# Two four-branch mixers: rotary key from the token product, a narrower first chunk, and y turns in other places

## Chip, cores, metric

One core of a Trainium2 chip runs the whole program in one launch. The metric is device microseconds (us) of that core. Engines: PE is TensorE, DVE is VectorE, ACT is ScalarE, POOL is GpSimd, and SP issues the DMAs.

## What is computed

Two networks run one after the other on 256 tokens of width 1024: first a block of two layers (feed-forward, mixer, feed-forward), then a block of two layers (mixer of four branches, feed-forward). The change lies in the second block's mixers alone. With `z = h @ w_in`, cut to what matters:

```
y_a = pool_mixer(pool_u)
y_b = chunk_band_attention(ca_q, ca_k, ca_v)
y_c = dsa_attention(sa_q, sa_k, sa_v, idx_q, idx_k, idx_w)   # top 64 keys of each query
y_d = mla_attention(cq, ckv, kr)                             # latents, key's rotary part from kr
k_rope = rope(kr, pos)            # 32 columns: kr * cos + swapped(kr) * sin, same for 4 heads
x = x + gt1 * (group_rmsnorm([y_a, y_b, y_c, y_d]) @ w_out)
```

`dsa_attention` scores every key with eight index heads, keeps the best 64 of them, and gives all others a large negative score. Everything is float32. Each large product is made of three matmuls on a split of both operands into a high and a low part (hi*hTh, lo*hTh, hi*hTl).

## The kernel before

Tokens stand in two tiles of 128 (t = 0 and 1; a step's last number is t). A mixer runs as a list of steps written out by hand, `ORDER2` for both four-branch mixers. PE executes its instructions in exactly that order. The order on DVE, ACT and POOL is made by a scheduler from priorities: `^60` after a step raises that of its instructions, and `@tp`, `@dn` and `@up` name the pool of PSUM banks (2 of tp, 4 of dn, 2 of up) from which the step takes its bank.

The steps that the prediction names, with their lines in the kernel before:

- `c0.t.i`, `c4.t.i` (`gemm_tok`, L477 to L480): products by tokens; c0 holds the latents cq and ckv, sa_v and idx_w, 456 columns wide. `ch.n.i` (`gemm_ch`, L491 to L493): products by channels, four tiles of 128 channels in chunk n, 24 matmuls in each quarter i.
- `lat.t` (L1265 to L1283) normalises the latents of one token tile into `cn`: DVE sums, POOL's power (L394), DVE scalings (L1278, L1279) and two small DVE copies. `lat_turn.t` (L1285) transposes `cn` on PE and ACT copies it to `cqT`. `mla_kv` makes keys and values from it.
- `dsa_in` (L1369) takes sa_k, sa_q and the index key out of chunk 1, and makes the rotary key there: chunk 1 held kr twice and its swapped form twice as one tile of 128 channels, which L1378 to L1380 turn into `mkT[64:128]`.
- `select.t`: PE makes index scores (L1420), ACT takes relu, DVE sums eight heads (L1429, L1431), and then DVE runs eight rounds of MAX8 and MATCH_REPLACE8 (L1436, L1437) and writes the penalty `pen` (L1439), which `dsa_score.t` adds to its scores (L1447).
- `name_pv.t` (`pv`, L846, then L849 on DVE) makes one branch's output y and `y_norm` normalises it: ACT squares (L865), DVE adds eps (L866), POOL's power (L394), DVE scales (L868). `name_y_turn.t` (L887) transposes y on PE; ACT (L892 or L898) and DVE (L893, or L901 and L902) split it into high and low parts.
- `w.t.k` (`down`, L501 to L504): product with row block k of `w_out` for token tile t. Blocks 6 and 7 are branch mla's, 0 and 1 pool's, 2 and 3 ca's, 4 and 5 dsa's.
- `L289` (ACT) and `L292` (DVE) split every weight tile into high and low parts.

A y of `pv` and the tiles `sc` and `pen` of `select` come from one pool of eight buffers (`s1`).

Of the kernel before, what the change touches and what calls it, by code (L numbers as in the profile page):

```python
# [10 lines left out]
ACTF = mybir.ActivationFunctionType  # L11
# [4 lines left out]
P = 128  # L16
# [8 lines left out]
def _columns(parts):  # L25
# [80 lines left out]
class Net:  # L106
# [374 lines left out]

    def gemm_ch(self, banks, unit, i):

        nc = self.nc
        hi, lo = unit
        for c in range(4):
            out = banks[c // 2][:, (c % 2) * 256:(c % 2) * 256 + 256]
            for kk in range(2):
                k = 2 * i + kk
                sl = slice(kk * 512 + c * 128, kk * 512 + (c + 1) * 128)  # L490
                nc.tensor.matmul(out, hi[:, sl], self.hTh[:, k], start=(k == 0 and c % 2 == 0), stop=False)  # L491
                nc.tensor.matmul(out, hi[:, sl], self.hTl[:, k], start=False, stop=False)  # L492
                nc.tensor.matmul(out, lo[:, sl], self.hTh[:, k], start=False, stop=(k == 7 and c % 2 == 1))  # L493

# [421 lines left out]

    def products(self, v, ks, mod, nxt, widths):
# [323 lines left out]
    def mixer2(self, l, mod, nxt):  # L1241
# [23 lines left out]
        def lat(t):  # L1265
# [224 lines left out]
        ops["c0"] = first("c0", 456, lat_out)  # L1490
        ops["c4"] = first("c4", 512, u_out)
# [24 lines left out]
    def body(self, n_sub, whole):  # L1516
# [72 lines left out]
def _constants():  # L1589
# [47 lines left out]
def layout(inp):  # L1637
# [125 lines left out]
    krs = np.concatenate([pc["kr"][..., 16:], pc["kr"][..., :16]], -1)
    out["mix2"] = mixer([pc["cq"], pc["ckv"], pc["sa_v"], pc["idx_w"]], 456,
                        [pc["pool_u"], pc["ca_v"], pc["sa_k"], pc["idx_k"], pc["kr"], pc["kr"], krs, krs,
                         pc["sa_q"], pc["idx_q"], pc["ca_q"], pc["ca_k"]], f["w_out_2"], ORDERS[2:])

# [39 lines left out]
```

## Time and profile before

| | |
|---|---|
| median of 3 runs | 1643.0 us (1641.3 to 1643.08) |
| the profiled execution's own time | 1641.78 us |
| its span in the trace | 1640.0 us |
| PE busy in it | 1601.5 us (98%) |
| PE's mean granted clock | 0.991 of full speed |

The span is what the trace covers; the execution's own time has some 1.8 us around it. In the trace PE's matmuls overlap each other, so a matmul's own duration is longer than its share of the engine's time: what one matmul costs is read from the distance between two starts. Times in the rows count from the span's start. The first four-branch mixer takes from about 1019 to 1135 us, the second from about 1328 to 1445 us.

### The profile page before, as it was taken

Reading aid. Unit: us, or ns where it says so; the run is one execution under the profiler, and the core shown is the slowest. Engines: PE = TensorE matmul, PEld = TensorE weight load, DVE = VectorE, ACT = ScalarE, POOL = GpSimd, SP = SyncE. Lnnn points to the kernel's source line nnn. Section 1 sums busy time; section 2 is a strip of 40 time slices with the busy share of each in tenths; the row PEclk is TensorE's granted clock in tenths of the full one; section 3 lists DMA queues with packets and bytes.
Section 4 is the critical chain, followed back from the end, with each engine's and each line's share of the span. In section 5 each row is a group of like instructions: output and inputs, shape, how many; then the busy total and the mean of one; then the engine's idle time right before and its main releaser. Section 6 shows DMA issues by size and latency. Waiting matters only on the chain.

```text
span 1640.0 us, 26615 instructions
## 1 busy us (share of the span) xinstructions
PE 1601.5 (98%) x10578; PEld 1446.6 (88%) x10578; DVE 1267.4 (77%) x2163; ACT 856.3 (52%) x1372; POOL 52.5 (3%) x62
## 2 busy tenths in 40 slices
PE   7999999999999999999899999999999999999998
PEld 6989988789998899989789998987899989789997
DVE  6988698688887978777688887687888776786554
ACT  5643558564445544458564445556544465474442
POOL 0000010000000000010000000001000010000000
PEclk9999999999999999999999999999999999999999
DMA  9889777369887798844369886434888854258550
GB/s 374 304 317 372 273 256 271 116 226 364 324 320 266 294 358 320 333 162 152 115 209 371 318 319 254 174 135 149 309 331 306 331 193 150 82 179 296 184 189 27
DMA packets 60623, 410.84 MB, mean 251 GB/s; under 512 B 6785, under 2 KB 7505, under 8 KB 14290
## 3 DMA queue, kind: packets, MB, share of 16 engines
q1 hardware_dynamic: 60208, 408.85, 67.6%
q8 instruction: 83, 1.36, 0.3%
q10 hardware_dynamic: 290, 0.29, 0.1%
q14 instruction: 42, 0.34, 0.1%
HBM read 408.02 MB, written 1.09 MB: 249 GB/s over the span
## 4 chain that ended last, share of the span: by engine, by line
PE 84%; DVE 9%; ACT 3%; DMA 2%; issue 1%; POOL 1%; SPq 0%; POOLq 0%; ACTq 0%; DVEq 0%
PE up L491 13%; PE up L492 13%; PE up L493 13%; PE dn L501 8%; PE dn L502 8%; PE dn L504 8%; DVE lo L292 2%; PE dn L477 2%; PE dn L480 2%; PE dn L478 2%; PE up L477 2%; PE up L480 2%; PE up L478 2%; PE dn L584 1%; DMA s<-in_w_ada 1%
## 5 line engine op out<-in xcount | busy, mean ns | idle before, releaser
L289 ACT ACTIVATE hi<-raw 128x1024 fp32r<-128x1024 f32 (+1 forms) x508 | 526.7, 1057 | 421.4 <-PE up L492 138.1
L292 DVE TENSOR_TENSOR lo<-raw,hi 128x1024 fp32r<-128x1024 f32 (+1 forms) x508 | 609.7, 1221 | 160.9 <-ACT hi L289 157.2
L491 PE MATMUL up<-hTh,hi 128*128 128x256 f32 x1920 | 540.8, 282 | 0.0
L492 PE MATMUL up<-hTl,hi 128*128 128x256 f32 x1920 | 538.0, 280 | 0.0
L493 PE MATMUL up<-hTh,lo 128*128 128x256 f32 x1920 | 537.9, 280 | 0.0
L491 PEld LDWEIGHTS up<-hTh,hi 128*128 128x128 f32 x1920 | 361.1, 188 | 3.2 <-issue 0.2
L492 PEld LDWEIGHTS up<-hTl,hi 128*128 128x128 f32 x1920 | 361.6, 188 | 2.1
L493 PEld LDWEIGHTS up<-hTh,lo 128*128 128x128 f32 x1920 | 361.5, 188 | 0.0
L345 DVE SCALAR_TENSOR_TENSOR raw<-raw,crow 128x1024 f32<-128x1024 f32 x224 | 267.5, 1221 | 2.6 <-DMA raw<-in_w_ada 2.3
L501 PE MATMUL dn<-hi,s 128*128 128x512 f32 x552 | 218.6, 396 | 0.0
L502 PE MATMUL dn<-lo,s 128*128 128x512 f32 x552 | 217.5, 394 | 0.0
L504 PE MATMUL dn<-hi,s 128*128 128x512 f32 x552 | 173.5, 394 | 0.0
L504 PEld LDWEIGHTS dn<-hi,s 128*128 128x128 f32 x552 | 103.7, 188 | 24.4
L502 PEld LDWEIGHTS dn<-lo,s 128*128 128x128 f32 x552 | 103.8, 188 | 21.4
L501 PEld LDWEIGHTS dn<-hi,s 128*128 128x128 f32 x552 | 103.7, 188 | 21.3
L676 ACT ACTIVATE s<-up 128x512 f32<-128x512 f32 (+1 forms) x59 | 32.0, 554 | 143.8 <-PE up L493 143.6
L677 DVE TENSOR_TENSOR s<-s,up 128x512 f32<-128x512 f32 (+1 forms) x59 | 36.8, 633 | 60.7 <-PE up L493 58.7
L477 PE MATMUL dn<-hi,hTh 128*128 128x512 f32 (+2 forms) x176 | 66.2, 380 | 0.3 <-DVE hTh L431 0.3
L426 ACT ACTIVATE s<-tp,shift,scale 128x128 f32<-128x128 f32 x144 | 52.0, 466 | 26.4 <-PE tp L439 26.4
L478 PE MATMUL dn<-lo,hTh 128*128 128x512 f32 (+2 forms) x176 | 65.1, 374 | 0.0
L480 PE MATMUL dn<-hi,hTl 128*128 128x512 f32 (+2 forms) x176 | 63.4, 375 | 0.0
L394 POOL TENSOR_TENSOR rs<-ms,mhalf 128x1 f32<-128x1 f32 x22 | 20.8, 948 | 1197.5 <-DVE ms L408 1197.5
(379 smaller groups left out, 2000.5 us busy)
## 6 DMA issues: line engine op xcount, KB each, us to landing
raw<-in_ffn SPq DMA_DIRECT2D x197, 1024.0 KB, 5.0
raw<-in_w_ada SPq DMA_DIRECT2D x64, 1024.0 KB, 6.3
raw<-in_mix SPq DMA_DIRECT2D x48, 1024.0 KB, 5.1
raw<-in_w_mod SPq DMA_DIRECT2D x48, 1024.0 KB, 7.0
s<-in_w_ada SPq DMA_DIRECT2D x16, 512.0 KB, 12.6
s<-gate SPq DMA_DIRECT2D x10, 512.0 KB, 9.1
raw<-in_mix SPq DMA_DIRECT2D x4, 1032.0 KB, 8.1
raw<-in_mix SPq DMA_DIRECT2D x4, 912.0 KB, 5.8
```

The costliest lines, as they stand in the source:

```text
L289: self.line("a", nc.scalar.activation(out=hi[:, :width], in_=r, func=ACTF.Copy))
L292: self.line("v", nc.vector.tensor_tensor(lo[:, :width], r, hi[:, :width].bitcast(F32), ALU.subtract))
L345: nc.vector.scalar_tensor_tensor(sl, sl, 1.0, self.crow, ALU.mult, ALU.mult, accum_out=dst[:, b:b + 1])
L477: nc.tensor.matmul(out, xh, hi[:, sl], start=(k == 0), stop=False)
L478: nc.tensor.matmul(out, xh, lo[:, sl], start=False, stop=False)
L480: nc.tensor.matmul(out, xl, hi[:, sl], start=False, stop=(k == 7))
L491: nc.tensor.matmul(out, hi[:, sl], self.hTh[:, k], start=(k == 0 and c % 2 == 0), stop=False)
L492: nc.tensor.matmul(out, hi[:, sl], self.hTl[:, k], start=False, stop=False)
L493: nc.tensor.matmul(out, lo[:, sl], self.hTh[:, k], start=False, stop=(k == 7 and c % 2 == 1))
L501: nc.tensor.matmul(banks[t, n], xh, hi[:, sl], start=first, stop=False)
L502: nc.tensor.matmul(banks[t, n], xh, lo[:, sl], start=False, stop=False)
L504: nc.tensor.matmul(banks[t, n], xl, hi[:, n * 512:n * 512 + 512], start=False, stop=last)
```

## The change

The rotary key is made by tokens now. c0 is 32 columns wider (488) and carries kr; `lat` makes kr * cos and the swapped kr * sin with three small DVE products and adds them, four times side by side, into columns 384 to 511 of `cn`; `lat_turn` transposes this fourth tile too, and DVE copies it into `mkT[64:128]`. Chunk 1 loses the tile that held kr, and has three tiles. `dsa_in` loses its three rotary instructions. The weights' layout follows.

`ORDER2` moves `mla_pv.1` and `mla_y_turn.1` to later places, `select.1` so to an earlier one, `dsa_y_turn.0` behind `ca_pv.1`, and `dsa_y_turn.1` behind `w.1.6`. Both mixers use it.

```diff
-gate_send@dn^150 gate_fetch mla_turn.1 ch.3.2 mla_pv.1@tp select.1^60 mla_y_turn.0 ch.3.3 pool_y_turn.0^-60
-mla_y_turn.1@tp^-60 ca_in w.0.6 ca_score.0@dn w.0.7 dsa_score.0 w.0.0 ca_score.1^-25 ca_turn.0@dn^25 w.0.1
-ca_pv.0@dn^150 dsa_turn.0@tp^60 dsa_score.1^-25 w.1.1 dsa_pv.0 ca_y_turn.0@tp ca_turn.1@dn^60 w.1.0 dsa_y_turn.0@tp
-ca_pv.1@dn^60 dsa_turn.1^150 w.0.2 w.0.5 w.0.4 w.0.3 ca_y_turn.1^-150 dsa_pv.1@dn^-25 w.1.7 w.1.3 dsa_y_turn.1@up
-w.1.6 resume.0 w.1.2 w.1.5 w.1.4
+gate_send@dn^150 gate_fetch mla_turn.1 ch.3.2 select.1^60 mla_y_turn.0 ch.3.3 ca_in mla_pv.1@tp pool_y_turn.0^-60
+w.0.6 ca_score.0@dn w.0.7 dsa_score.0 mla_y_turn.1@tp^-60 w.0.0 ca_score.1^-25 ca_turn.0@dn^25 w.0.1
+ca_pv.0@dn^150 dsa_turn.0@tp^60 dsa_score.1^-25 w.1.1 dsa_pv.0 ca_y_turn.0@tp ca_turn.1@dn^60 w.1.0 ca_pv.1@dn^60
+dsa_y_turn.0@tp dsa_turn.1^150 w.0.2 w.0.5 w.0.4 w.0.3 ca_y_turn.1^-150 dsa_pv.1@dn^-25 w.1.7 w.1.3 w.1.6
+dsa_y_turn.1@up resume.0 w.1.2 w.1.5 w.1.4
...
-        for c in range(4):
+        for c in range(tiles):
...
+            rope = self.con("rope_k")[:, t * 64:t * 64 + 64]
+            kr = self.sm(64, "kr", 2)
+            nc.vector.tensor_tensor(kr[:, 0:32], ps[:, 456:488], rope[:, 0:32], ALU.mult)
+            nc.vector.tensor_tensor(kr[:, 32:48], ps[:, 472:488], rope[:, 32:48], ALU.mult)
+            nc.vector.tensor_tensor(kr[:, 48:64], ps[:, 456:472], rope[:, 48:64], ALU.mult)
+            nc.vector.tensor_tensor(cn[:, 384:512].rearrange("p (o n) -> p o n", o=4),
+                                    kr[:, 0:32].rearrange("p (o n) -> p o n", o=1).to_broadcast([P, 4, 32]),
+                                    kr[:, 32:64].rearrange("p (o n) -> p o n", o=1).to_broadcast([P, 4, 32]), ALU.add)
...
-            for c in range(3):
+            for c in range(4):
                 nc.tensor.transpose(pt[:, c * 128:(c + 1) * 128], cn[:, c * 128:(c + 1) * 128], self.ident)
...
+            nc.vector.tensor_copy(mkT[64:128, :, t * 128:(t + 1) * 128],
+                                  pt[64:128, 384:512].rearrange("p (o n) -> p o n", o=1).to_broadcast([64, 4, 128]))
...
-            return b, [(b[:, 0:456], 0, 456)]
+            return b, [(b[:, 0:488], 0, 488)]
...
-            nc.vector.tensor_tensor(k1[0:64], c1[0][0:64, 256:512], self.con("rope_k")[0:64], ALU.mult)
-            nc.vector.tensor_tensor(k2[0:64], c1[0][64:128, 256:512], self.con("rope_k")[64:128], ALU.mult)
-            nc.vector.tensor_tensor(mkT[64:128],
-                                    k1[0:64].rearrange("p (o n) -> p o n", o=1).to_broadcast([64, 4, 256]),
-                                    k2[0:64].rearrange("p (o n) -> p o n", o=1).to_broadcast([64, 4, 256]), ALU.add)
...
-                    width = (1032 if i < 6 else 912) if name == "c0" else 1024
+                    width = (1032 if i < 6 else 976) if name == "c0" else 768 if i > 5 and name == "ch1" else 1024
```

How the engines' queues change is read from the built programs. The first place is PE's queue in the first mixer, from `dsa_score.0` on, first before the change. L793 with L1447 is `dsa_score.0`, L501 to L504 with s_10334 is `w.0.0`, and the next L793 is `ca_score.1`.

```order
L793 MATMUL dn<-s_10332,s_10333 128x128 x2
L1447 MATMUL dn<-s_11004,identr 128x256
L501 MATMUL up<-hi,s_10334 128x512
L502 MATMUL up<-lo,s_10334 128x512
L501 MATMUL up<-hi,s_10334 128x512
L502 MATMUL up<-lo,s_10334 128x512
L504 MATMUL up<-hi,s_10334 128x512 x2
L793 MATMUL dn<-s_10337 128x256 x4
```

The same place with the change, where L1451 is the former L1447, and L887 is `mla_y_turn.1`, the transposes of y tile s_11174:

```order
L793 MATMUL dn<-s_10332,s_10333 128x128 x2
L1451 MATMUL dn<-s_10990,identr 128x256
L887 MATMUL tp<-cst,s_11174 128x128 x2
L501 MATMUL up<-hi,s_10334 128x512
L502 MATMUL up<-lo,s_10334 128x512
L501 MATMUL up<-hi,s_10334 128x512
L502 MATMUL up<-lo,s_10334 128x512
L504 MATMUL up<-hi,s_10334 128x512 x2
L793 MATMUL dn<-s_10337 128x256 x4
```

`mla_y_turn.1` now stands between `dsa_score.0` and `w.0.0`; before, it stood directly behind `pool_y_turn.0`, ahead of `w.0.6`, `ca_score.0`, `w.0.7` and `dsa_score.0`.

The second place is DVE's queue around `mla_pv.1`'s output, first before the change. s_11095 is that y, s_10956 and s_11004 are `sc` and `pen` of `select.0`, s_11104 is `sc` of `select.1`, s_10335 holds the mla branch's split y.

```order
L1437 MATCH_REPLACE s_10956<-m_11001,s_10956 128x128
L1439 TENSOR_SCALAR s_11004<-s_10956 128x128
L849 TENSOR_TENSOR s_11095<-tp,rsum 128x256
L1429 TENSOR_SCALAR s_11104<-s_11108,iwn 128x256
L1431 SCALAR_TENSOR_TENSOR s_11104<-s_11108,iwn,s_11104 128x256
L866 TENSOR_SCALAR ssy<-ssy 128x1
L1431 SCALAR_TENSOR_TENSOR s_11104<-s_11115,iwn,s_11104 128x256
L868 TENSOR_SCALAR s_11095<-s_11095,rsy 128x256
```

With the change y is s_11174, `select.1` has s_11072 for `sc` and s_11126 for `pen`, and the lines of `select` are four higher (L1440 is the former L1436, L1443 the former L1439). These rows stand together:

```order
L1440 MAX m_11117<-s_11072 128x8
L1441 MATCH_REPLACE s_11072<-m_11117,s_11072 128x256
L1440 MAX m_11120<-s_11072 128x8
L1441 MATCH_REPLACE s_11072<-m_11120,s_11072 128x256
L1440 MAX m_11123<-s_11072 128x8
L1441 MATCH_REPLACE s_11072<-m_11123,s_11072 128x256
L1443 TENSOR_SCALAR s_11126<-s_11072 128x256
L849 TENSOR_TENSOR s_11174<-tp,rsum 128x256
L866 TENSOR_SCALAR ssy<-ssy 128x1
L868 TENSOR_SCALAR s_11174<-s_11174,rsy 128x256
```

The three instructions of `mla_pv.1`'s y (L849, L866, L868) stood behind `select.0` and ahead of `select.1`'s rounds; now they stand behind the last round of `select.1`. The second mixer's queues show both moves in the same way.

The third place is DVE's queue in `lat`, from the first token tile to be normalised to the second, first before the change (ms_10526 belongs to the second tile).

```order
L1280 COPY sv<-up 128x64
L1281 TENSOR_SCALAR iwn<-up 128x8
L1274 TENSOR_SCALAR ms_10526<-ss_10522 128x1
L1275 TENSOR_SCALAR ms_10526<-ss_10522 128x1
L292 TENSOR_TENSOR lo<-raw,hi 128x1024
```

With the change, where L1283 to L1286 are the rotary instructions, L1289 is the former L1281, and ms_10531 belongs to the second tile:

```order
L1280 COPY sv<-up 128x64
L1283 TENSOR_TENSOR kr<-up,cst 128x32
L1284 TENSOR_TENSOR kr<-up,cst 128x16
L1285 TENSOR_TENSOR kr<-up,cst 128x16
L1289 TENSOR_SCALAR iwn<-up 128x8
L1286 TENSOR_TENSOR s_10517<-kr 128x128
L1274 TENSOR_SCALAR ms_10531<-ss_10527 128x1
L1275 TENSOR_SCALAR ms_10531<-ss_10527 128x1
L292 TENSOR_TENSOR lo<-raw,hi 128x768
```

Four instructions of the first tile came in ahead of the second tile's chain; the second tile has its own four behind its scalings.

## Rows read from the trace of the kernel before

**Rows 1.** Page, part 1: busy time, share of the span, instructions.

```profile
PE 1601.5 (98%) x10578; PEld 1446.6 (88%) x10578; DVE 1267.4 (77%) x2163; ACT 856.3 (52%) x1372; POOL 52.5 (3%) x62
```

**Rows 2.** Page, part 4: the chain that ended last, by engine.

```profile
PE 84%; DVE 9%; ACT 3%; DMA 2%; issue 1%; POOL 1%; SPq 0%; POOLq 0%; ACTq 0%; DVEq 0%
```

**Rows 3.** Waits of PE, 1020 to 1150 us: waiter, releaser, total, times, longest.

```profile
PE tp L887 <- DVE s L893: 2.2, 1, 2.2
PE tp L887 <- DVE s L868: 1.0, 1, 1.0
PE dn L1447 <- DVE s L1439: 0.6, 1, 0.6
PE up L887 <- DVE s L868: 0.4, 1, 0.4
```

**Rows 4.** Timeline of PE (start, duration, instruction): mla_y_turn.1, w.0.0, w.1.1, both mixers.

```profile
1093.60 0.44 PE L887 MATMUL tp<-cst,s 128*128 128x128 f32 x2 [2.20 <-DVE s L893]
...
1099.75 0.39 PE L501 MATMUL up<-hi,s 128*128 128x512 f32 x1
...
1109.12 0.40 PE L501 MATMUL dn<-hi,s 128*128 128x512 f32 x1
...
1402.11 0.44 PE L887 MATMUL tp<-cst,s 128*128 128x128 f32 x2 [2.21 <-DVE s L893]
...
1409.79 0.39 PE L501 MATMUL up<-hi,s 128*128 128x512 f32 x1
...
1419.13 0.39 PE L501 MATMUL dn<-hi,s 128*128 128x512 f32 x1
```

**Rows 5.** Timeline of DVE: both selections' ends in mixer one, the first's in two.

```profile
1089.44 0.23 DVE L1439 TENSOR_SCALAR s<-s 128x128 fp32r<-128x128 f32 x1
...
1091.74 0.35 DVE L868 TENSOR_SCALAR s<-s,rsy 128x256 f32<-128x256 f32 x1 [0.44 <-POOL rsy L394]
...
1105.98 0.42 DVE L1436 MAX8 m<-s 128x8 f32<-128x256 f32 x1
...
1106.51 0.41 DVE L1437 MATCH_REPLACE8 s<-m,s 128x256 f32<-128x256 f32 x1
1106.96 0.29 DVE L1439 TENSOR_SCALAR s<-s 128x256 fp32r<-128x256 f32 x1
...
1397.95 0.23 DVE L1439 TENSOR_SCALAR s<-s 128x128 fp32r<-128x128 f32 x1
```

**Rows 6.** Timeline of PE: c0, c4, lat_turn, chunk 1.

```profile
1025.21 0.37 PE L477 MATMUL up<-hi,hTh 128*128 128x456 f32 x1
...
1031.24 0.36 PE L480 MATMUL up<-hi,hTl 128*128 128x456 f32 x1
1031.44 0.40 PE L477 MATMUL dn<-hi,hTh 128*128 128x512 f32 x1
...
1036.79 0.39 PE L480 MATMUL dn<-hi,hTl 128*128 128x512 f32 x1
1037.10 0.84 PE L1289 MATMUL tp<-cst,s 128*128 128x128 f32 x6
1037.70 0.36 PE L491 MATMUL up<-hTh,hi 128*128 128x256 f32 x1
...
1040.47 0.28 PE L493 MATMUL up<-hTh,lo 128*128 128x256 f32 x1
```

**Rows 7.** Timeline of DVE: the end of lat for the second token tile.

```profile
1036.87 0.34 DVE L1279 TENSOR_SCALAR s<-up,r 128x128 f32<-128x128 f32 x1
1037.13 0.22 DVE L1280 COPY sv<-up 128x64 f32<-128x64 f32 x1
```

**Rows 8.** Timeline of POOL: the two powers of lat.

```profile
1032.93 0.71 POOL L394 TENSOR_TENSOR r<-ms,mhalf 128x2 f32<-128x2 f32 x1 [12.22 <-DVE ms L1275]
1034.82 1.61 POOL L394 TENSOR_TENSOR r<-ms,mhalf 128x2 f32<-128x2 f32 x1 [1.18 <-DVE ms L1275]
```

**Rows 9.** Windows: us, PE, PEld, DVE, ACT, POOL busy; granted clock, DMA share, GB/s.

```profile
1405.00:1406.00 1.00, 1.00 (x9) 0.78 (x9) 0.00 (x1) 0.00 (x0) 0.00 (x0) 0.50 0.08 16
```

More of the change, by code (lines that the diff above doesn't have):

```diff
@@ L33 @@
 CONST_COLS, N_CONST = _columns((
-    ("ident", 128), ("tri_le", 128), ("gt", 256), ("sb_tri", 128), ("sb_keep", 128), ("rope_q", 256), ("rope_k", 256)))
+    ("ident", 128), ("tri_le", 128), ("gt", 256), ("sb_tri", 128), ("sb_keep", 128), ("rope_q", 256), ("rope_k", 128)))
 MASK_COLS, N_MASK = _columns((("causal", 128), ("past", 128), ("chunk", 128)))
@@ L480, in gemm_tok, with gemm_ch @@
                 nc.tensor.matmul(out, xl, hi[:, sl], start=False, stop=(k == 7))
-    def gemm_ch(self, banks, unit, i):
+    def gemm_ch(self, banks, unit, i, tiles=4):
         nc = self.nc
         hi, lo = unit
-        for c in range(4):
+        for c in range(tiles):
             out = banks[c // 2][:, (c % 2) * 256:(c % 2) * 256 + 256]
@@ L489, in gemm_ch @@
                 k = 2 * i + kk
-                sl = slice(kk * 512 + c * 128, kk * 512 + (c + 1) * 128)
+                sl = slice((kk * tiles + c) * 128, (kk * tiles + c + 1) * 128)
                 nc.tensor.matmul(out, hi[:, sl], self.hTh[:, k], start=(k == 0 and c % 2 == 0), stop=False)
                 nc.tensor.matmul(out, hi[:, sl], self.hTl[:, k], start=False, stop=False)
-                nc.tensor.matmul(out, lo[:, sl], self.hTh[:, k], start=False, stop=(k == 7 and c % 2 == 1))
+                nc.tensor.matmul(out, lo[:, sl], self.hTh[:, k], start=False, stop=(k == 7 and (c % 2 == 1 or c == tiles - 1)))
     def down(self, banks, t, x, unit, first, last, halves=(0, 1)):
@@ L915, in perform, with products @@
             self.side.pop(0)()
-    def products(self, v, ks, mod, nxt, widths):
+    def products(self, v, ks, mod, nxt, widths, tiles={}):
         def first(name, width, outs):
@@ L933, in ch @@
             banks, units = v["ch", n]
-            self.gemm_ch(banks, units[i], i)
+            self.gemm_ch(banks, units[i], i, tiles.get(n, 4))
             self.free(1)
@@ L1374, in dsa_in @@
                         sakT[d * 64:d * 64 + 64, i], c1[0][i * 64:i * 64 + 64, 0:256])
-            nc.scalar.activation(out=saqT, in_=c1[1].rearrange("p (c n) -> p c n", c=2), func=ACTF.Copy, scale=0.125)
-            k1 = self.s1()
-            k2 = self.s1()
-            nc.vector.tensor_tensor(k1[0:64], c1[0][0:64, 256:512], self.con("rope_k")[0:64], ALU.mult)
-            nc.vector.tensor_tensor(k2[0:64], c1[0][64:128, 256:512], self.con("rope_k")[64:128], ALU.mult)
-            nc.vector.tensor_tensor(mkT[64:128],
-                                    k1[0:64].rearrange("p (o n) -> p o n", o=1).to_broadcast([64, 4, 256]),
-                                    k2[0:64].rearrange("p (o n) -> p o n", o=1).to_broadcast([64, 4, 256]), ALU.add)
+            nc.scalar.activation(out=saqT[:, 0], in_=c1[0][:, 256:512], func=ACTF.Copy, scale=0.125)
+            nc.scalar.activation(out=saqT[:, 1], in_=c1[1][:, 0:256], func=ACTF.Copy, scale=0.125)
         def mla_score(t):
@@ L1482, in mixer2 @@
             self.y_tiles(k, False)
-        first, ops = self.products(v, blocks(ORDERS[2 + l])[1], mod, nxt, {1: "up", 2: "dn", 3: "up"})
+        first, ops = self.products(v, blocks(ORDERS[2 + l])[1], mod, nxt, {1: "up", 2: "dn", 3: "up"}, {1: 3})
         ops.update({f.__name__: f for f in (lat, lat_turn, us, mla_q, mla_kv, pool_d, pool_y, dsa_in, mla_score, index_in,
@@ L1489, in mixer2 @@
             ops[name + "_y_turn"] = lambda t, name=name, k=k: y_turn(name, t, k)
-        ops["c0"] = first("c0", 456, lat_out)
+        ops["c0"] = first("c0", 488, lat_out)
         ops["c4"] = first("c4", 512, u_out)
@@ L1608, in _constants @@
     put("rope_q", np.concatenate([np.ones((64, S), np.float32), cos32, sin32]) * sc)
-    put("rope_k", np.concatenate([cos32, cos32, sin32, sin32]))
+    put("rope_k", np.concatenate([f[:, t * 128:(t + 1) * 128].T for t in range(2) for f in (cos32, sin32)], 1))
     return c
@@ L1732, in mixer @@
         first = kp(np.concatenate(first, -1), width)[:, 0]
-        rest = kp(np.concatenate(rest, -1), 512)
+        rest = [kp(w, w.shape[-1])[:, 0] for w in (np.concatenate(chunk, -1) for chunk in rest)]
         layers = []
@@ L1736, in mixer @@
             chunks, ks = blocks(order)
-            parts = {"c0": first[i], "c4": rest[i, 0], **{f"ch{n}": rest[i, n] for n in range(1, 4)}}
+            parts = {"c0": first[i], "c4": rest[0][i], **{f"ch{n}": rest[n][i] for n in range(1, 4)}}
             layers.append(np.concatenate([parts[c] for c in chunks]
@@ L1744, in layout @@
     part = [w[..., o[i]:o[i + 1]] for i in range(9)]
-    out["mix1"] = mixer([part[5], part[6], part[8]], 516, [part[7], part[4], part[0], part[1], part[2], part[3]], f["w_out"],
+    out["mix1"] = mixer([part[5], part[6], part[8]], 516, [[part[7], part[4]], [part[0]], [part[1]], [part[2], part[3]]], f["w_out"],
                         ORDERS[:2])
@@ L1762, in layout @@
         pos += n
[L1763 to L1766, printed above, removed]
+    out["mix2"] = mixer([pc["cq"], pc["ckv"], pc["sa_v"], pc["idx_w"], pc["kr"]], 488,
+                        [[pc["pool_u"], pc["ca_v"]], [pc["sa_k"], pc["idx_k"], pc["sa_q"]], [pc["idx_q"]],
+                         [pc["ca_q"], pc["ca_k"]]], f["w_out_2"], ORDERS[2:])
     uq = f["mla_w_uq_2"]
```

## The prediction, as it went on record

> **What bounds the kernel now.** I read the page's busy table first: PE is busy for 98% of the span, DVE for 77% [rows 1]. The chain that ended last says the same, 84% of it is PE [rows 2]. So an edit counts by what it adds to or takes from PE's queue, and by the places where that queue waits. PE's waits in the first four-branch mixer come next: four, together 4.2 us, all for DVE [rows 3]; the second mixer lists the same four. Their places come from PE's timeline. The 2.2 us are `mla_y_turn.1`, started at 1093.60, which waited for DVE to empty the tp bank of an earlier y turn (L893) [rows 4]. The 0.6 us are `dsa_score.1`, for the penalty of `select.1` (L1439). The 1.0 and 0.4 us are `dsa_y_turn.0` and `dsa_y_turn.1`, for a scaled y (L868). The last view is DVE's timeline between the two selections' ends, 1089.44 and 1106.96: 17.5 us [rows 5]. The reader should see that PE reached `dsa_score.1` only 0.6 us before that selection was done. The hand-written order had about 7 us of PE work (from `w.0.0`, at 1099.75) ahead of that wait, and this work needed nothing of `select.1`.
>
> **Chunk 1 and c0.** Per mixer, chunk 1 loses one of four tiles: 24 matmuls of 256 columns. The 24 of one quarter start from 1037.70 to 1040.47, 0.12 us apart [rows 6], so 2.9 us go. c0 grows by 32 columns in 48 matmuls (8 blocks, 3 products, 2 token tiles). 30 matmuls of 456 columns start 0.208 us apart (1025.21 to 1031.24) and 24 of 512 start 0.233 apart (1031.44 to 1036.79) [rows 6]. Between them 32 columns cost 0.014 us, and 48 of these 0.7 us. Two more transposes cost 0.1 us each, by six in the 0.6 us from 1037.10 to 1037.70 [rows 6]: 0.2 us.
>
> [...]
>
> **The rotary key in lat.** Before, `lat_turn` started at 1037.10, while the last scaling it needs ran from 1036.87 for 0.34 us [rows 6, 7]. So DVE has no slack here. The change puts four DVE instructions of the first token tile ahead of the second tile's chain, and the second tile's own four ahead of the transpose that needs them. No row has them. The 64-column copy was 0.22 us long and the scaling of 128 columns 0.34, and DVE goes on somewhat sooner than these end (0.26 us after the scaling's start) [rows 7]. I take three small ones 0.1 apart and the wide one at 0.3: 0.6 us per tile, 1.3 us for two, less 0.3 us of transposes that can go first: PE waits 1.0 us more per mixer. The bounds are nothing (if the second tile's waits swallow it) and 1.9 us (all at full duration: 1.1 us per tile, less 0.3).
>
> The two powers of `lat` took 0.71 and 1.61 us on POOL [rows 8]. [...]
>
> The copies of the key into `mkT` stand on DVE ahead of the tp banks' release for `mla_kv`; the first quarter of chunk 1 lies between, 2.2 us long, and covers them (uncovered, up to 1 us). The three rotary instructions that leave `dsa_in` save PE nothing: none of its waits is there [rows 3]. Narrower weights (L289, L292) shorten engines that PE does not wait for in this stretch. So PE comes to the selections 2.9 - 0.7 - 0.2 - 1.0 = 1.0 us sooner per mixer.
>
> **The y of mla, second token tile: the term that decides.** In the changed order `mla_pv.1` stands behind `select.1`, and in DVE's queue its L849, L866 and L868 stand behind the last round of `select.1`. `mla_y_turn.1` needs that y, and it stands on PE between `dsa_score.0` and `w.0.0`. Behind it in PE's queue are all of `w.0.0`, `ca_score.1`, `ca_turn.0`, `w.0.1`, `ca_pv.0`, `dsa_turn.0` and `dsa_score.1`. This is the work that used to cover `select.1`.
>
> When does PE get there? Before, it was free for `mla_y_turn.1` at 1093.60 - 2.20 = 1091.40, and from its start to `w.0.0` went 1099.75 - 1093.60 = 6.15 us [rows 4], of which 0.2 are its own transposes. The same work now comes first: 1091.40 + 5.95 - 1.0 = 1096.35.
>
> When is y ready? `select.0` is done at 1089.44 - 1.0 = 1088.44. DVE's stretch to the end of `select.1` was 17.5 us. Out of it go L849, L866, L868 with its 0.44 us wait, two L893 and the four row maxima of `ca_score.1` with their sum, together some 3 us by these rows and their like. Against that, five of the eight rounds now run with nothing between. MAX8 and MATCH_REPLACE8 last 0.42 and 0.41 us [rows 5], and each has to wait for the one before; in the interleaved rows the two advance DVE by 0.75 us, bare I take 0.97, so 1.1 us come back. Some 0.9 us more I allow for L893s and a split that now wait for ACT. That leaves 16.5 us; the bounds are 14.5 (nothing comes back) and 17.5. From the end of a selection to the end of its following L868 took 1091.74 + 0.35 - 1089.44 = 2.65 us [rows 5]. So `mla_y_turn.1` starts at 1088.44 + 16.5 + 2.65 = 1107.6: PE waits 11.2 us, in place of 2.2.
>
> Behind it, from `w.0.0` to `w.1.1` went 1109.12 - 1099.75 = 9.37 us with the 0.6 us wait [rows 3, 4]; that wait is gone, 8.76 us remain. `w.1.1` starts at 1107.6 + 0.2 + 8.8 = 1116.6, against 1109.12: **7.5 us later**. In the second mixer the first selection ended at 1397.95 and `w.1.1` came at 1419.13 [rows 4, 5]: 1397.95 - 1.0 + 16.5 + 2.65 + 0.2 + 8.8 = 1425.1, **6.0 us later**.
>
> **TensorE's clock.** [...] I take 1.5 us each, 3.0 in all; bounds 0 and 3 each.
>
> **The dsa turns.** `dsa_y_turn.0` behind `ca_pv.1` and `dsa_y_turn.1` behind `w.1.6` have 1.4 us of matmuls or more ahead of them that they did not have, so the waits of 1.0 and 0.4 us go [rows 3]. But `w.0.5` needs the first one's split, and DVE's queue now has two splits L292 and a copy ahead of it; I put 1.3 us of new waiting there. Together -0.1 us per mixer; bounds -1.4 and +0.6.
>
> **Sum**, against the profiled execution's own time, 1641.78 us (its span 1640.0; the runs' median 1643.0 is 1.2 above it): 7.5 + 6.0 + 3.0 - 0.2 = +16.3 us, **1658.1 us**, 0.9% above the median. No change can be told from less than 0.2%, some 3.3 us, in this kernel.
>
> **Rivals.**
>
> *The turn does not hold PE (faster).* This is what the order would bring if DVE reached y early: all four waits gone, 4.2 us per mixer, the second's clock fall too (1.5), and 1.0 per mixer from chunk 1: 1641.8 - 8.4 - 1.5 - 2.0 = 1629.9 us. It decides at the length of DVE's stretch: the first mixer breaks even when `mla_y_turn.1` starts at 1109.12 - 8.8 - 0.2 = 1100.1, so with a stretch of 1100.1 - 2.65 - 1088.44 = 9.0 us. The rows show 17.5, and eight rounds alone are 6 us at the interleaved 0.75 [rows 5]. Chance 0.04.
>
> *The clock stays low over all that follows the wait (much slower).* At half clock throughout, the 8.8 us behind each wait would take up to twice as long, 8.8 us for each mixer in place of 1.5: 1672.7. Half of that price gives 1664.1. For it speaks the length of the wait; against it, that the engine returned to full speed within the 7.68 us of [rows 4]. Chance 0.12.
>
> *No change that can be told.* The transfer of y behind the selection would have to be paid by the gains, which needs 4 us of waiting in place of 11.2 per mixer, by a stretch near 9 us as above: 1642 us. Chance 0.03.
>
> My case has 0.81. Its own range is 1650 to 1665: DVE's stretch 2 us shorter in both mixers (-4) and no clock term (-3) at one end; 1 us longer (+2), clock at its upper bound (+3) and the key's bound (+1.8) at the other. The 8 in 10 range is 1650 to 1667, which takes in the half-price clock case. Faster by over 0.2% has 0.04, within 0.2% 0.03, slower 0.93.
>
> **What would show it.** PE's waits with the change should list L887 behind DVE L868 with some 11 us, once per mixer, and no L893 of 2.2 us. On DVE, 14.5 to 17.5 us should lie between the two selections' last instructions. The granted clock should read 0.50 behind the wait. The distance from the first c0 matmul to chunk 1's end should shrink by about 1 us. The prediction is wrong if that long wait is under 5 us, or if other work stands between.

## The result, and the profile with the change

The changed kernel takes 1665.95 us (median of 4 runs, 1664.64 to 1667.14), the kernel before 1643.04 in the same runs: a ratio of 1.0143, 95% interval 1.0131 to 1.0155. The forecast was 1658.1 with a range of 1650 to 1667: slower, as forecast, and 7.9 us above the value.

The page of the profiled execution (1667.14 us by itself), parts 1 and 4, answers to [rows 1] and [rows 2]. PE has 1.9 us more busy time (1603.4 against 1601.5) in a span 25.4 us longer (1665.4 against 1640.0), so nearly all of the time went into waits:

```profile
PE 1603.4 (96%) x10534; PEld 1443.8 (87%) x10534; DVE 1269.5 (76%) x2177; ACT 856.6 (51%) x1374; POOL 49.8 (3%) x62
...
PE 81%; DVE 11%; ACT 3%; DMA 2%; issue 2%; POOL 1%; SPq 0%; POOLq 0%; ACTq 0%; DVEq 0%
```

PE's waits in the first mixer (waiter, releaser, total, times, longest), as in [rows 3]; the second mixer lists the same:

```profile
PE tp L887 <- DVE s L868: 10.0, 1, 10.0
PE dn L501 <- DVE hTh L901: 2.4, 1, 2.4
PE tp L831 <- ACT s L836: 0.7, 1, 0.7
PE up L501 <- DVE s L1467: 0.4, 1, 0.4
PE tp L1297 <- DVE s L1286: 0.4, 1, 0.4
```

The four waits of before are gone. The first new one is the forecast wait of `mla_y_turn.1` for its y; the second, at `w.1.5`, was not forecast. PE's timeline at the places of [rows 4], `mla_y_turn.1`, `w.0.0` and `w.1.1`, then `mla_y_turn.1` and `w.1.1` of the second mixer:

```profile
1109.03 0.69 PE L887 MATMUL tp<-cst,s 128*128 128x128 f32 x2 [10.03 <-DVE s L868]
1109.37 0.78 PE L501 MATMUL up<-hi,s 128*128 128x512 f32 x1
...
1119.34 0.40 PE L501 MATMUL dn<-hi,s 128*128 128x512 f32 x1
...
1430.27 0.69 PE L887 MATMUL tp<-cst,s 128*128 128x128 f32 x2 [10.03 <-DVE s L868]
...
1441.96 0.39 PE L501 MATMUL dn<-hi,s 128*128 128x512 f32 x1
```

DVE's timeline, as in [rows 5]: the ends of both selections (L1443), then the y for which PE waits (L849, L868); the last two rows are the ends of the second mixer's selections:

```profile
1090.14 0.23 DVE L1443 TENSOR_SCALAR s<-s 128x128 fp32r<-128x128 f32 x1
...
1106.48 0.29 DVE L1443 TENSOR_SCALAR s<-s 128x256 fp32r<-128x256 f32 x1
1106.68 0.42 DVE L849 TENSOR_TENSOR s<-tp,rsum 128x256 f32<-128x256 f32 x1
...
1108.62 0.35 DVE L868 TENSOR_SCALAR s<-s,rsy 128x256 f32<-128x256 f32 x1 [0.73 <-POOL rsy L394]
...
1411.37 0.23 DVE L1443 TENSOR_SCALAR s<-s 128x128 fp32r<-128x128 f32 x1
...
1427.72 0.29 DVE L1443 TENSOR_SCALAR s<-s 128x256 fp32r<-128x256 f32 x1
```

The stretch between the selections is 16.34 us (1106.48 - 1090.14) and 16.35 in the second mixer; y is ready 2.49 us behind the selection's last instruction.

To see where the time came in, the mixers are cut at rows that both kernels have. One is L439, the eight transposes by which a layer's start is resumed. PE's timeline of before, ahead of mixer one, at `resume.0` near its end, and in the next layer; then the same three of the changed kernel:

```profile
1011.23 1.03 PE L439 MATMUL tp<-cst,s 128*128 128x128 f32 x8
...
1130.49 1.03 PE L439 MATMUL tp<-cst,s 128*128 128x128 f32 x8
...
1143.90 1.04 PE L439 MATMUL tp<-cst,s 128*128 128x128 f32 x8
```

```profile
1012.80 1.03 PE L439 MATMUL tp<-cst,s 128*128 128x128 f32 x8
...
1140.57 1.04 PE L439 MATMUL tp<-cst,s 128*128 128x128 f32 x8
...
1158.17 1.04 PE L439 MATMUL tp<-cst,s 128*128 128x128 f32 x8
```

Differences of such starts, in us (before, changed, difference):

| stretch on PE | mixer one | mixer two |
|---|---|---|
| first L439 to `select.0`'s scores | 64.44, 63.58, -0.86 | 64.35, 63.50, -0.85 |
| to the last instruction of `dsa_score.0` | 23.86, 22.24, -1.62 | 25.39, 22.25, -3.14 |
| to `w.1.1` | 9.59, 20.72, +11.13 | 9.56, 22.11, +12.55 |
| to `resume.0` | 21.37, 21.23, -0.14 | 21.37, 21.21, -0.16 |
| to the next layer's L439 | 13.41, 17.60, +4.19 | 13.38, 16.04, +2.66 |
| sum | 132.67, 145.37, +12.70 | 134.05, 145.11, +11.06 |

The mixers cost 23.8 us together; another 1.6 us of the profiled execution lie ahead of the first mixer (1012.80 - 1011.23), where the change has nothing. I take them for the executions' own difference: in all traces but that of `own_buffers` below, this first L439 starts between 1010.8 and 1014.5.

The windows (us, busy time of PE, PEld, DVE, ACT, POOL, granted clock, DMA share, GB/s) show TensorE's clock in and behind the long waits. It fell to 0.50 while PE waited, and came back 3 us after PE's work began in mixer one (1109.03) and 6 us after it in mixer two (1430.27):

```profile
1102.00:1109.00 7.00, 0.00 (x0) 0.00 (x0) 5.31 (x19) 1.79 (x10) 0.55 (x1) 0.50 0.00 0
1109.00:1111.00 2.00, 1.97 (x6) 1.68 (x7) 0.41 (x2) 0.74 (x2) 0.00 (x0) 0.50 0.00 0
...
1112.00:1113.00 1.00, 1.00 (x9) 0.71 (x8) 0.00 (x0) 0.00 (x0) 0.00 (x0) 1.00 0.00 0
...
1430.00:1436.00 6.00, 5.73 (x19) 3.90 (x20) 1.36 (x6) 0.73 (x2) 0.00 (x0) 0.50 0.00 0
```

Last the unforecast place. `dsa_y_turn.1` ran on PE at 1140.35 and needed no wait any more; `w.1.5`, which reads its split, then waited 2.36 us (PE, ACT and DVE in turn):

```profile
1145.36 0.50 PE L501 MATMUL dn<-hi,hTh 128*128 128x512 f32 x1 [2.36 <-DVE hTh L901]
```

```profile
1141.52 0.35 ACT L898 ACTIVATE s<-up,cols 128x128 f32<-128x128 f32 x1
1141.77 2.90 ACT L426 ACTIVATE s<-tp,shift,scale 128x128 f32<-128x128 f32 x8
1144.51 0.42 ACT L898 ACTIVATE s<-up,cols 128x128 f32<-128x128 f32 x1
```

```profile
1139.42 3.49 DVE L292 TENSOR_TENSOR lo<-raw,hi 128x1024 fp32r<-128x1024 f32 x3
...
1145.02 0.29 DVE L901 CAST hTh<-s 128x256 fp32r<-128x256 f32 x1
```

The second half of the y's copy (L898) stands on ACT behind all eight copies of `resume.0` (L426, 2.9 us), and the split L901 on DVE starts when it is done, behind three weight splits (L292) and the splits of `resume.0` itself, which need the same copies. In mixer one a fall of the clock follows as well: the granted clock is 0.54 from 1146 to 1147 and 0.50 from 1147 to 1149.

### The profile page after: what moved, and what is told of

It reads as the page before. It is cut to its first block, busy times and chain, and to the rows that moved or that the text cites. A ratio compares the mean times of both kernels' runs of the same rounds, so it can differ in the third digit from the quotient of the medians.

```text
span 1665.4 us, 26529 instructions
## 1 busy us (share of the span) xinstructions
PE 1603.4 (96%) x10534; PEld 1443.8 (87%) x10534; DVE 1269.5 (76%) x2177; ACT 856.6 (51%) x1374; POOL 49.8 (3%) x62
## 4 chain that ended last, share of the span: by engine, by line
PE 81%; DVE 11%; ACT 3%; DMA 2%; issue 2%; POOL 1%; SPq 0%; POOLq 0%; ACTq 0%; DVEq 0%
PE up L491 13%; PE up L492 13%; PE up L493 13%; PE dn L501 8%; PE dn L502 8%; PE dn L504 8%; DVE lo L292 3%; PE up L477 2%; PE up L480 2%; PE dn L477 2%; PE up L478 2%; PE dn L480 2%; PE dn L478 2%; PE dn L793 1%; DMA s<-in_w_ada 1%
## 5 line engine op out<-in xcount | busy, mean ns | idle before, releaser
L289 ACT ACTIVATE hi<-raw 128x1024 fp32r<-128x1024 f32 (+2 forms) x508 | 525.8, 1055 | 428.3 <-PE up L492 139.9
L292 DVE TENSOR_TENSOR lo<-raw,hi 128x1024 fp32r<-128x1024 f32 (+2 forms) x508 | 607.6, 1216 | 159.0 <-ACT hi L289 156.4
L501 PE MATMUL dn<-hi,s 128*128 128x512 f32 x552 | 218.5, 396 | 0.0
L504 PE MATMUL dn<-hi,s 128*128 128x512 f32 x552 | 173.5, 394 | 0.0
L504 PEld LDWEIGHTS dn<-hi,s 128*128 128x128 f32 x552 | 103.7, 188 | 24.4
L501 PEld LDWEIGHTS dn<-hi,s 128*128 128x128 f32 x552 | 103.7, 188 | 21.4
L426 ACT ACTIVATE s<-tp,shift,scale 128x128 f32<-128x128 f32 x144 | 52.2, 469 | 26.9 <-PE tp L439 26.9
```

Source lines behind the costliest of these rows:

```text
L289: self.line("a", nc.scalar.activation(out=hi[:, :width], in_=r, func=ACTF.Copy))
L292: self.line("v", nc.vector.tensor_tensor(lo[:, :width], r, hi[:, :width].bitcast(F32), ALU.subtract))
L501: nc.tensor.matmul(banks[t, n], xh, hi[:, sl], start=first, stop=False)
L504: nc.tensor.matmul(banks[t, n], xl, hi[:, n * 512:n * 512 + 512], start=False, stop=last)
```

## The experiments

The theory: the late y of `mla_pv.1`, with the clock behind its wait, costs some 9 us a mixer; the place of `dsa_y_turn.1` 2.7 us, and 1.5 more where the clock falls; the key gives 0.85 back. The rivals: the key is what costs; the late place of `mla_y_turn.1` on PE costs by itself; what follows the waits is slow for reasons other than the clock. "Mixers" are the sums of the table above. The diffs of `ORDER2` show the steps around those that move, without its line breaks; `...` stands for what is left out.

**The key alone**: the changed kernel with `ORDER2` of before.

```diff
-gate_send@dn^150 gate_fetch mla_turn.1 ch.3.2 select.1^60 mla_y_turn.0 ch.3.3 ca_in mla_pv.1@tp pool_y_turn.0^-60
+gate_send@dn^150 gate_fetch mla_turn.1 ch.3.2 mla_pv.1@tp select.1^60 mla_y_turn.0 ch.3.3 pool_y_turn.0^-60
...
```

> The rotary key by tokens with the order of before. Theory (the order costs the time, the key gains a little): PE comes 0.85 us sooner to select.0 in each mixer, as in the trace of the changed kernel, so 1643.0 - 1.7 = 1641.3 us (1640.3 to 1642.5); the four waits of before stay. Rival (the key is what costs: DVE's extra work in lat makes the selections late): 1648 us or more.

1642.21 us, ratio 0.9996 (0.9987 to 1.0005). The rival falls: the key costs nothing. Its gain can't be told from nothing here and is smaller than expected, though PE comes 0.89 and 0.78 us sooner to `select.0`. In the traced execution mixer one gives it back: behind the same 2.2 us wait of `mla_y_turn.1` the clock fell, which it did not in the execution of before. The first row is of this run, where the turn starts at 1092.54, the second of before, where it starts at 1093.60:

```profile
1092.00:1096.00 4.00, 3.46 (x12) 2.39 (x14) 3.35 (x11) 2.37 (x6) 0.00 (x0) 0.57 0.00 0
```

```profile
1094.00:1098.00 4.00, 3.91 (x22) 2.38 (x20) 4.00 (x19) 1.35 (x5) 0.00 (x0) 1.00 0.01 4
```

In mixer two the clock fell in both executions (0.63 over 1402 to 1406 here, 0.57 over 1403 to 1407 before), and this run's mixer is 0.63 us shorter (133.42 against 134.05).

**The order alone**: the kernel before with the changed `ORDER2`.

```diff
-gate_send@dn^150 gate_fetch mla_turn.1 ch.3.2 mla_pv.1@tp select.1^60 mla_y_turn.0 ch.3.3 pool_y_turn.0^-60
+gate_send@dn^150 gate_fetch mla_turn.1 ch.3.2 select.1^60 mla_y_turn.0 ch.3.3 ca_in mla_pv.1@tp pool_y_turn.0^-60
...
```

> The key of before with the changed order. Theory: in each mixer some 9.3 us from the late y of mla with its clock fall, and 4.2 and 2.7 us from the last steps (w.1.5 waiting for the y of dsa), and nothing gained: 1643.0 + 18.6 + 6.9 = 1668.5 us (1666 to 1670). Rival (the key costs): 1650 us or less.

1668.16 us, ratio 1.0158 (1.0145 to 1.0172). The time is as the theory has it; the waits of 10.0 and 2.4 us are there in both mixers without the key.

**`dsa_y_turn.1` back**:

```diff
-w.1.7 w.1.3 w.1.6 dsa_y_turn.1@up resume.0 w.1.2 w.1.5 w.1.4
+w.1.7 w.1.3 dsa_y_turn.1@up w.1.6 resume.0 w.1.2 w.1.5 w.1.4
```

> The changed kernel with dsa_y_turn.1 ahead of w.1.6 again. Theory (its place alone makes w.1.5 wait 2.4 us, and the clock falls behind that): 1666.0 - 6.9 = 1659 us (1657 to 1661), no wait of a w step on L901 at the mixer's end. Rival (that wait only passes on DVE's lateness from the long wait before it): 1664 us or more, the wait stays.

1660.36 us, ratio 1.0110 (1.0096 to 1.0124), 5.6 less than the change. That is inside the theory's range, though its sum had 6.9. The wait at `w.1.5` is gone and the last stretch is 13.41 and 13.38 us again, as before. The rival falls.

**`resume.0` behind `w.1.2`**, `dsa_y_turn.1` left where the change has it:

```diff
-w.1.6 dsa_y_turn.1@up resume.0 w.1.2 w.1.5 w.1.4
+w.1.6 dsa_y_turn.1@up w.1.2 resume.0 w.1.5 w.1.4
```

> The changed kernel with resume.0 behind w.1.2, dsa_y_turn.1 still behind w.1.6. Theory (w.1.5 waits because the second half of the y's copy stands behind the eight copies of resume.0 on ACT): the wait of 2.4 us falls to 0.3 at most, 2 x 2.2 us, and one clock fall of 1.5 us with it: 1666.0 - 5.9 = 1660 us (1658.5 to 1662). Rival (three weight splits L292 ahead of it on DVE make it late anyway): the wait stays over 1.5 us, 1664 us or more.

1660.99 us, ratio 1.0108 (1.0095 to 1.0122). PE's waits list what is left at `w.1.5`:

```profile
PE dn L501 <- DVE hTh L901: 0.2, 1, 0.2
```

So `resume.0` ahead of it was what held it, not the three weight splits on DVE, which are still ahead of L901 here. Both halves of L898 now run together on ACT (from 1141.42) and the copies L426 behind them; the splits of `resume.0` on DVE have moved behind L901 as well, and this run doesn't part the two.

**`mla_pv.1` back ahead of `select.1`**, `mla_y_turn.1` late as in the change:

```diff
-select.1^60 mla_y_turn.0 ch.3.3 ca_in mla_pv.1@tp pool_y_turn.0^-60
+mla_pv.1@tp select.1^60 mla_y_turn.0 ch.3.3 ca_in pool_y_turn.0^-60
```

> The changed kernel with mla_pv.1 ahead of select.1 again, and mla_y_turn.1 late as in the change. Theory (the wait comes from the place of L849 in DVE's queue): no 10 us wait at mla_y_turn.1; but PE then reaches dsa_score.1 some 2.2 us sooner than before while DVE does not, so 2.8 us of waiting stands there; with the last steps' cost, 1643.0 - 1.7 + 6.9 - 2 for dsa_y_turn.0 = 1646 us (1644 to 1650). Rival (the late place on PE is what costs, by what then stands behind it): 1658 us or more.

1651.36 us, ratio 1.0054 (1.0038 to 1.0069): the 10 us wait is gone, so the rival falls, but the time is 5 us over the theory's. The wait that was to stand at `dsa_score.1` is shared with `w.0.6`, which waits for the copies of `ca_in`:

```profile
PE dn L501 <- DVE hTh L901: 2.4, 1, 2.4
PE up L501 <- DVE s L1467: 2.0, 1, 2.0
PE dn L1451 <- DVE s L1443: 1.0, 1, 1.0
```

In the traced execution mixer one takes 134.4 us, and behind these waits the matmuls of 512 columns start 0.23 us apart (1093.65, 1093.88; 1108.49, 1108.72; 1134.50, 1134.73), which is their distance at a clock of 1.00; mixer two takes 141.9 with nearly the same waits. There the clock read 0.50 to 0.58 from 1403 to 1410, around and behind the wait at `w.0.6`, 0.50 to 0.52 from 1420 to 1425 behind the one at `dsa_score.1`, and behind the one at `w.1.5` the matmuls of 512 columns start 0.43 us apart (1452.73, 1453.16), as in the change at 0.50.

**Own buffers**: every order as in the change, but y and the scratch tile of its norm leave the pool `s1`.

```diff
-        y = self.s1()
+        y = self.s.tile([P, 256], F32, tag="sy", name="sy", bufs=2)
...
-        junk = self.s1()
+        junk = self.s.tile([P, 256], F32, tag="sj", name="sj", bufs=1)
```

> The changed kernel, every order as in the change, but the y of a branch and the scratch tile of its norm have buffers of their own (two and one) in place of the pool that sc and pen of select share. In the built queue L849, L866 and L868 of mla's second token tile then stand ahead of select.1's rounds. Theory (the wait comes from the place in DVE's queue, which the shared pool's order of allocation sets, and not from PE's order): no wait of 10 us at mla_y_turn.1, waits of 1 to 3 us at dsa_score.1 or w.0.6 in its place, the last steps' cost as in the change: 1649 us (1646 to 1653). Rival (mla_y_turn.1 stands too late on PE): 1660 us or more.

1662.29 us, ratio 1.0115 (1.0100 to 1.0131). By its number this is the rival's case, but the time decides nothing, since the layers ahead became slower: the first L439 is at 1020.63, 7.8 us later than in the change. In the mixers the 10 us wait is gone and 3.3 us at `dsa_score.1` are in its place. So the next kernel gives buffers of their own to `mla_pv.1` alone (one for y and one for the scratch tile):

```diff
-        y = self.s1()
+        y = self.s.tile([P, 256], F32, tag="sy", name="sy", bufs=1) if own else self.s1()
...
-        junk = self.s1()
+        junk = self.s.tile([P, 256], F32, tag="sj", name="sj", bufs=1) if own else self.s1()
...
-            v[name + "y", t] = self.y_norm(self.pv(t, pT, rs, val))
+            v[name + "y", t] = self.y_norm(self.pv(t, pT, rs, val, (name, t) == ("mla", 1)), (name, t) == ("mla", 1))
```

> As own_buffers, but only the y of mla's second token tile and its scratch tile leave the shared pool, so that the layers ahead keep their queues. Theory (the wait comes from the place in DVE's queue): the two mixers take 141 and 138 us from their first L439 to the next layer's, as in own_buffers, where the change has 145.4 and 145.1: 1666.0 - 11.5 = 1654.5 us (1652 to 1657), 3.3 us of waiting at dsa_score.1 in place of 10. Rival (the late place of mla_y_turn.1 on PE is what costs): 1660 us or more.

1652.28 us, ratio 1.0059 (1.0045 to 1.0072); the mixers take 139.3 and 137.4. The time is the theory's, and the rival falls. PE's waits in mixer one (2.3 us at `dsa_score.1`, where 3.3 were expected), and DVE's timeline there with y ready at 1098.07, 10.6 us ahead of the selection's end:

```profile
PE dn L501 <- DVE hTh L901: 2.4, 1, 2.4
PE dn L1451 <- DVE s L1443: 2.3, 1, 2.3
```

```profile
1095.50 0.42 DVE L849 TENSOR_TENSOR sy<-tp,rsum 128x256 f32<-128x256 f32 x1
...
1097.72 0.35 DVE L868 TENSOR_SCALAR sy<-sy,rsy 128x256 f32<-128x256 f32 x1
...
1108.42 0.29 DVE L1443 TENSOR_SCALAR s<-s 128x256 fp32r<-128x256 f32 x1
```

PE's order is the change's. Only the buffers differ, and L849 goes ahead of the rounds. The place in DVE's queue is the cause, and the shared pool sets it.

**PE kept busy in the wait**: 84 transposes of the identity ahead of the two of `mla_y_turn.1`; DVE's, ACT's and POOL's queues are unchanged.

```diff
         ps = self.bank("tp")
+        for i in range(idle):
+            nc.tensor.transpose(ps[:, 0:128], self.ident, self.ident)
```

> The changed kernel with 84 transposes of the identity, into the bank of mla_y_turn.1, ahead of its own two: PE is busy for most of the 10 us in which it waited, and all else is as in the change. Theory (behind the wait the same instructions run at the clock's lower level): from mla_y_turn.1 to w.1.1 9.0 us in both mixers, where the change has 10.3 and 11.7, granted clock 1.00 there: 1666.0 - 4.1 = 1662 us (1660 to 1663.5). Rival (they are slow for other reasons, as the weights' reading or DVE's lateness): 1665 us or more.

1663.07 us, ratio 1.0123 (1.0109 to 1.0137). From `mla_y_turn.1` to `dsa_score.1`'s first penalty PE took 8.48 and 9.86 us in the change (to 1117.51 and 1440.13), and 7.13 and 7.11 here, with the clock at 1.00:

```profile
1108.96 0.38 PE L889 MATMUL tp<-cst,s 128*128 128x128 f32 x2
...
1116.09 0.50 PE L1453 MATMUL dn<-s,identr 128*128 128x512 f32 x1
```

```profile
1109.00:1117.00 8.00, 8.00 (x47) 5.97 (x45) 3.14 (x15) 4.28 (x14) 0.55 (x1) 1.00 0.33 113
...
1429.00:1437.00 8.00, 8.00 (x48) 6.02 (x47) 3.10 (x14) 4.28 (x14) 0.41 (x1) 1.00 0.00 0
```

So the falls cost 1.35 and 2.75 us, and the rival falls. The time fell by 2.9 us and not by 4.1; in the traced execution, mixer two is only 0.9 us shorter than in the change (144.22 against 145.11), since the transposes themselves met a low clock there (0.50 from 1419 to 1421) and ran past the wait, to 1429.20, where y was ready at 1427.30.

**`mla_y_turn.1` behind `w.1.1`**, and `dsa_y_turn.1` back:

```diff
-dsa_score.0 mla_y_turn.1@tp^-60 w.0.0 ... dsa_score.1^-25 w.1.1 dsa_pv.0
+dsa_score.0 w.0.0 ... dsa_score.1^-25 w.1.1 mla_y_turn.1@tp^-60 dsa_pv.0
```

> The changed kernel with mla_y_turn.1 behind w.1.1 and dsa_y_turn.1 ahead of w.1.6 again; mla_pv.1 stays behind select.1. Theory (between the two selections' ends DVE is full, so PE can come no sooner to dsa_score.1 than in the kernel before, however little it waits ahead of that): no 10 us wait, in its place some 3 us at dsa_score.1; 1641 us (1638 to 1643.5). Rival (with the turn out of the way PE keeps the 2.2 us that it waited before): no wait over 1 us at dsa_score.1, 1636 us or less.

1648.21 us, ratio 1.0034 (1.0021 to 1.0048). That is beyond the theory's 1638 to 1643.5. The stretch on DVE is 17.3 us again (1088.83 to 1106.12) and PE waits at `dsa_score.1` for its end, 1.7 us where some 3 were expected. It gets there 1.1 us sooner than before, counted from the first L439, of which the key gives 0.9. So DVE's stretch sets that place, as the theory has it. It missed what came behind: 1.4 us at L831 for a copy of an earlier y turn on ACT (L898), and the clock at 0.50 from 1107 to 1111.

**More cover**: as that, with `w.1.1` and `w.1.0` ahead of `dsa_score.1` and `mla_y_turn.1` behind `ca_pv.1`.

```diff
-dsa_score.1^-25 w.1.1 mla_y_turn.1@tp^-60 dsa_pv.0 ca_y_turn.0@tp ca_turn.1@dn^60 w.1.0 ca_pv.1@dn^60
+w.1.1 w.1.0 dsa_score.1^-25 dsa_pv.0 ca_y_turn.0@tp ca_turn.1@dn^60 ca_pv.1@dn^60 mla_y_turn.1@tp^-60
```

> As the kernel with mla_y_turn.1 behind w.1.1, but w.1.1 and w.1.0 (2.8 us of PE's work that needs nothing of the selection) stand ahead of dsa_score.1, and mla_y_turn.1 behind ca_pv.1. Theory: PE's work covers DVE's stretch, wait at dsa_score.1 under 1 us, 2.5 us less per mixer than before, 1.7 us from the key, no fall of the clock: 1636 us (1633 to 1641). Rival (mla's y, now behind select.1 and its followers on DVE, comes too late for any place ahead of w.1.7): over 2 us of waiting at mla_y_turn.1, 1642 us or more.

1649.64 us, ratio 1.0041 (1.0029 to 1.0054): the time is in the rival's range, but both missed the mechanism. Nothing waits at `dsa_score.1` or `mla_y_turn.1`, and the waits have gone to the steps behind, most of them for a bank of `dn`, in a stretch where the clock then reads 0.50 from 1118 to 1122. Mixer one:

```profile
PE dn L846 <- DVE s L834: 1.4, 1, 1.4
PE dn L831 <- DVE ssy L866: 1.1, 1, 1.1
PE tp L831 <- ACT s L898: 1.0, 1, 1.0
```

**The key and `dsa_y_turn.0` behind `ca_pv.1`**, all else in the order of before:

```diff
-w.1.0 dsa_y_turn.0@tp ca_pv.1@dn^60 dsa_turn.1^150
+w.1.0 ca_pv.1@dn^60 dsa_y_turn.0@tp dsa_turn.1^150
```

> The rotary key by tokens, the order of before, and dsa_y_turn.0 behind ca_pv.1 as in the change. Theory: its wait of 1.0 us goes and 0.7 us at dsa_turn.1 (L831) and 0.3 at w.0.5 come, as in the trace of the change: nothing, 1642.2 us (1641 to 1643). Rival (the new waits belong to the lateness of the change alone): 1640.2 us.

1640.79 us, ratio 0.9990 (0.9981 to 0.9999). The median lies between the rival's 1640.2 and the theory's range, so the time doesn't decide between them. The trace does: the 1.0 us wait went and 0.7 us at L831 came, and the stretch from `w.1.1` to `resume.0` is 21.28 us in both mixers against 21.37. This move is worth nothing that can be told, as the theory has it. The traced execution had no fall of the clock behind the 2.2 and 2.4 us waits (1.00 from 1094 to 1098 and from 1402 to 1406), so it keeps the key's gain. It is the fastest version run, by 0.1% of the time before.

**`w.1.1` ahead of `dsa_score.1` besides**:

```diff
-dsa_score.1^-25 w.1.1 dsa_pv.0
+w.1.1 dsa_score.1^-25 dsa_pv.0
```

> As dsa0_moved, and w.1.1 ahead of dsa_score.1. Theory: the 0.6 us wait for select.1 is covered, 1.2 us less: 1641 us (1639.5 to 1642.5). Rival (w.1.1's two banks of dn are missed by the steps behind it, as the waits of more_cover for L834 and L866 show): 1643.5 us or more.

1643.70 us, ratio 1.0005 (0.9996 to 1.0014). The 0.6 us wait is gone, and 1.1 us at L831 for DVE's L866 came: the time is the rival's, and the wait is one that it names. Of the 2.9 us above `dsa0_moved`, how much these waits cost is not shown: in the traced execution here the matmuls of 512 columns behind the waits of `mla_y_turn.1` start 0.42 to 0.43 us apart (1093.78, 1094.21; 1404.17, 1404.59), as in the change at a clock of 0.50, and there they start 0.23 us apart (1094.47, 1094.70; 1402.30, 1402.53).

## Why the prediction was right, and which term was not

**Key and chunk 1**: forecast 1.0 us sooner per mixer, measured 0.86 and 0.85. c0 took 0.71 more (forecast 0.7); transposes with their wait 0.8 (from 1039.38 to 1040.78, against [rows 6]) in place of 1.2; chunk 1 with what follows up to `select.0` gave 2.4 in place of 2.9. The second power of `lat`, which has no term in the sum, went from 1.61 [rows 8] to 1.35 us while the split beside it (L292) went from 1.22 to 0.95; no run shows whether the one made the other.

**The late y**: forecast to start `mla_y_turn.1` at 1107.6, measured 1109.03, or 1107.5 without the 1.57 us from ahead of the mixer. The stretch was 16.3 us (forecast 16.5), the way from the selection's last instruction to y 2.5 (2.65). The wait was 10.0 (11.2), since PE itself came 1.1 us later than forecast, 0.7 of it two waits at `w.0.6` for `ca_in`. `own_buffers_mla` shows that DVE's queue made the wait. `w.1.1` came 8.65 and 8.56 us later (10.22 less 1.57; 22.83 less the 14.27 that lay ahead of mixer two); forecast, with the clock, 9.0 and 7.5.

**The clock**: forecast 1.5 behind each of the two waits, measured by `busy_wait` 1.35 and 2.75. The 1.5 us are what mixer two of before, with its clock at 0.50 from 1405 to 1406 [rows 9], took longer than mixer one from `mla_y_turn.1` to `w.0.0`: 1409.79 - 1402.11 = 7.68 us against 6.15 [rows 4]. That a wait of some 11 us brings such a fall in both mixers was my estimate, which no row shows; both waits of 10.03 us brought it (0.50 from 1102 to 1109 and from 1423 to 1430). At 0.50 the matmuls of 512 columns start 0.43 us apart (1109.94, 1110.37), against 0.233 at 1.00 [rows 6].

**The dsa turns: the step that failed.** Forecast -0.1 us per mixer, with +0.6 as the upper bound; measured -0.14 and -0.16 up to `resume.0`, and +4.19 and +2.66 behind it. That "the waits of 1.0 and 0.4 us go" held. But for `dsa_y_turn.1` I looked only at what PE has ahead of the turn, not at what the turn's copies have ahead of them on ACT; the wait of their reader, `w.1.5`, stood at nothing. Behind `w.1.6` the step is next to `resume.0`, and one of its two copies fell behind eight others; `resume_later` shows that this neighbour makes the wait. The mixers of the traced execution cost 23.8 us, 7.5 more than the sum's 16.3. Some 6.75 of these are this term, and 0.7 came ahead of it: mixer two 1.1 over its forecast at `w.1.1`, by its longer fall of the clock, and mixer one 0.35 under.

**The rivals and the range**: the turn held PE, so the faster case is out. 1664.1, for a clock at half price, lies near the result by accident: the falls behind the long waits cost 4.1 us in all, not 8.8. So it is partly luck that the result lies inside the range, 1.05 us below its upper end: my case's own range ended at 1665, below the result, and the wider one was drawn to take in a clock at half price, which did not come. What filled that room was the dsa term, well outside its bound of +0.6.

**Slips in the working**: two tiles at 0.6 us are 1.2 and not 1.3 us, half the clock's price gives 1663.9 and not 1664.1, and the terms named for the lower end give 1651 and not 1650. None of them changes the account.

## What to carry to other kernels

A step that moves takes its instructions to a new place on every engine: where its result is read soon after, look at the queue of each engine that makes it (here DVE's for y, ACT's for the last copies), not only at the engine that waits. Buffers shared with a long chain can put a short chain behind it: here y was ready 2.5 us behind the selection's last instruction, and 10.6 us ahead of it with buffers of its own. Where another engine is full (DVE between the two selections), taking a wait out of one place on PE mostly moved it to the next in these runs (in four of them the 10.0 us of `mla_y_turn.1` went, and 1.0 to 3.3 us came at `dsa_score.1`).

## What the runs showed of the hardware that was not expected

The same wait of 2.2 to 2.4 us at `mla_y_turn.1` was followed by a fall of TensorE's clock in some traced executions and not in others: in mixer two of the kernel before [rows 9] but not in its mixer one (1.00 from 1094 to 1098), in both mixers with the key alone (0.57 and 0.63) and, by the distance of the matmuls' starts, of `w11_ahead` (0.42 to 0.43 us), in neither mixer of `dsa0_moved` (1.00). Where it fell, the work from that turn to the end of `dsa_score.0` took 7.0 to 7.5 us and elsewhere 5.9, so the fall cost 1.1 to 1.5 us, more than the key gains. A wait of 0.98 us (`busy_wait`, mixer two) was followed by a clock of 0.50 too (1419 to 1421), the same wait in its mixer one was not (1.00 from 1099 to 1109), and behind the two waits of 10.03 us it came back after 3 us of work in one mixer and 6 in the other. Why they differ is open: no run here tells it.
